# Weight slots filled out of turn, one split moved to the DVE, and an unpermuted sum at the end of a hybrid SSM, attention and MoE block

## The chip, the core and the metric

The kernel runs on one core of a Trainium2 chip. The metric is the device time of one execution in microseconds (us), as the median of several runs. TensorE is called PE in the profile (its weight loads PEld), VectorE DVE, ScalarE ACT, GpSimd POOL, SyncE SP. SP issues nearly all transfers here, in one queue.

## The reference, cut to what matters

One layer works on 272 tokens (16 meta tokens and 256 of input) of width 1024: a diagonal state-space branch and a sliding-window attention branch, both gated, are added to the stream; then a mixture of 32 experts with the top 4 for each token, and a last norm.

```python
proj = hn @ w_in[layer]                      # u, q, k, v and two gates
y = s5_ssm(u, ...); z = gelu(y); ssm_out = z * sigmoid(z @ w_glu + b_glu)
attn_out = sliding_window_attention(q, k, v, sinks)
h = h + (sigmoid(g_ssm) * (ssm_out @ w_br_ssm) + sigmoid(g_attn) * (attn_out @ w_br_attn)) @ w_out
...
gu = xb @ w_gate_up[e] + b_gate_up[e]        # 1024 x 2048 for each expert
g, up = clipped halves of gu
hid = g * sigmoid(1.702 * g) * (up + 1.0)
y = hid @ w_down[e] + b_down[e]              # 1024 x 1024 for each expert
...
return rmsnorm(h, norm_final)[:, N_META:]
```

Everything is float32. The weights of one expert are 8 MB (gate and up) and 4 MB (down), so 32 experts read 384 MB.

## The kernel before, in words

**The ring.** All weights go through one ordered list, `ring.todo`, into slots of 1024 KB (2048 floats on each of 128 partitions). First come single blocks (w_in, w_glu, w_br_ssm, w_br_attn, w_out), then the experts' units of four slots each: two units of gate and up for each expert (rows for k = 0 to 3 and 4 to 7), and one unit of down, which stands behind the gate and up units of the next expert. The order of units is therefore expert 0 (two), expert 1 (two), down of expert 0, expert 2 (two), down of expert 1, and so on. `pump` issues the head of the list as soon as there are free slots for it; a unit may be filled in one transfer of four slots, in pairs that lie beside each other in a "quad", or singly into two or more slots that stand alone. `done` gives a slot back when its last reader has been issued, and the transfer that refills it waits on SP for that reader. `retire` takes a slot out of the ring. With `patient` set, a unit waits for a whole quad; `most = 2` forbids that.

**The slots.** `r0` gives five slots (four of them later a quad, printed as r), and the quads ZScgtX, QYWgt and ws four each. Three slots stand alone in memory that other stages use: `s_acc` (in aA, where `acc` lies afterwards, opened in turn 8 of the block loop), `s_y` (late_, where the experts' outputs `ys` lie afterwards, opened in turn 15), and one more in aA, opened in turn 22. `s_acc` and `s_y` are retired after the block loop; the third stays in the ring. Before the change `s_acc` holds a block of w_br_ssm and then the rows for k = 2 of expert 0, the third one the rows for k = 3, and `s_y` a block of w_br_attn and then a row of expert 1's second unit.

**The block loop** (turns n = 0 to 41) works off 40 blocks: 8 each of the second gate, w_glu, w_br_ssm, w_br_attn and w_out. Each block's weights are split in two float32r parts: `hi` (ACT) copies, `lo` (L928) subtracts, and PE multiplies with both. The turns 0 to 13 also carry the steps of the attention: `scores` on PE, `normalise` of the step before and `maxima` on DVE, `exps` on ACT, `transposes` of the step before on PE with copies on ACT, `values` on PE. `bias_parts` (turns 0 to 2) splits the experts' bias into three bf16 parts on ACT, with a subtraction on DVE (L1024) between them. Program order in a turn sets the order on each engine.

**The experts.** For each expert, PE runs `gate_up` (k = 0 to 7, 32 products in pairs of column halves), then `down` of the expert before. Within `gate_up`, `mid(k)` places `hid_T` of the expert before, every second expert a `combine` of a pair of experts into `acc`, and steps of `group`, a generator that gathers the tokens of the next pair (`gather`, four steps) and makes its gate matrix (`gates_T`). For expert 0 every `mid(k)` takes one step of `group(0)`, of which two were taken before.

**The order of columns.** w_gate_up and w_down are read so that columns in the MoE stay in a permuted order ("p (n c)" against "p (c n)"): `down` turns the order back when it copies its result from PSUM (L1439, L1440), and the last stage writes its result through permuted views (L1526, L1527). The weights of the last norm are spread over the partitions by two products in PSUM (`nf_banks`, L1509) in the last expert's `gate_up`.

**The end.** `down(31)` has `combine_one` for the pair's first half in its turns c = 1 and c = 3 (two products, two adds into `acc`), and a second time for the other half after it. Then come squares (ACT), root (DVE, POOL), weigh (DVE), scale (ACT and DVE) and the stores.

Of the kernel before, what the change touches and what calls it, by code (L numbers as in the profile page):

```python
# [93 lines left out]


class Ring:
# [4 lines left out]
    def __init__(self, eng):  # L101
        self.eng = eng
        self.todo, self.held, self.free, self.used, self.patient, self.most = [], [], [], 0, False, 4

# [28 lines left out]
    def pump(self):  # L133
        while self.free and self.todo:
            u = self.todo[0]
            alone = [sl for sl in self.free if sl.quad is None]
# [8 lines left out]
            left = u.n - u.at  # L145
# [58 lines left out]
def hybrid_block(ctx: ExitStack, tc: tile.TileContext, x, meta, norm_mix, w_in, lam_re, lam_im, log_dt,  # L204
# [67 lines left out]
    for c in (6, 7):  # L272
        ring.add(dn_half(n_exp - 1, c))

# [926 lines left out]
    for n in range(B + 2):  # L1201
# [21 lines left out]
        if n == 0:  # L1223
            blocks[2].lo(G)
# [104 lines left out]
    keep_clock(bank("y", "idle"), b3[:, :128], b3[:, :416], 2)  # L1329
# [5 lines left out]
    keep_clock(bank("y", "idle"), b3[:, :128], b3[:, :416], 2)  # L1335
# [78 lines left out]

    cols2 = lambda t: t.rearrange("p (n c) -> p c n", c=4)
    rows2 = lambda t: t.rearrange("p (c n) -> p c n", c=4)

    def down(hT_, wc, selr, y, odd, mid=None, two=False):
# [20 lines left out]
        S.activation(rows2(y[:64, odd]), cols2(py[0][:64]), AF.Copy)  # L1439
        V.tensor_copy(rows2(y[64:, 1 - odd]), cols2(py[1][64:]))  # L1440

    def combine_one(gT, y, b, then=None):


        for t in range(2):
            pcs = [bank("y", "pc"), bank("t", "pc")]
            for hf in range(2):
                r = slice(64, 128) if hf != b else slice(0, 64)
                T.matmul(pcs[hf], gT[r, hf, t], y[r, hf], start=True, stop=True, tile_position=(r.start, 0))
            for hf in range(2):  # L1450
                cs_ = slice(512 * hf, 512 * hf + 512)
                V.tensor_tensor(acc[:, t, cs_], acc[:, t, cs_], pcs[hf], op=OP.add)
            if then:
                then(t)
            yield
# [3 lines left out]
    def combine(gT, y, then=None):  # L1459
        for t in range(2):  # L1460
            for hf in range(2):
# [3 lines left out]
                V.tensor_tensor(acc[:, t, cs_], (acc if started else xt)[:, t, cs_], pc, op=OP.add)  # L1465
# [13 lines left out]
    def group(e0, n):  # L1479
# [6 lines left out]
        if e0 == 0:  # L1486
            gates()
# [32 lines left out]
    def weigh(t, nf):  # L1520

        V.tensor_tensor(spare[t][:, :512], acc[:, t, :512], nf[0], op=OP.mult)

    def scale(t, nf):
# [7 lines left out]
    def last(nf):  # L1532
        for t in range(2):
            root(t)
            weigh(t, nf)
            scale(t, nf)
# [11 lines left out]
    more, nf = None, []  # L1548
    for e in range(n_exp + 1):
        f = e - 1  # L1550
        if e == n_exp - 1:
            nfr = pm.tile([128, 512], F32, tag="gT", name="nfr", bufs=3)
            for hf in range(2):
                S.dma_start(out=nfr[32 * hf:32 * hf + 1], in_=norm_final[512 * hf:512 * hf + 512].rearrange("(o d) -> o d", o=1))
        if e < n_exp:
# [3 lines left out]
            def mid(k):  # L1559
# [4 lines left out]
                if k == 4 and e == n_exp - 1:  # L1564
                    nf.extend(nf_banks())
# [3 lines left out]
            ring.patient, ring.most = 8 < e < 29, 4 if e < 29 else 2  # L1569
# [7 lines left out]
        if f >= 0:  # L1577
            if f % 2 == 0:
                assert ring.idle(s_y) or f
# [3 lines left out]
            def mid_d(c):  # L1583
                if e == n_exp - 1 and c == 3:
                    HID[e] = hid_T(HID[e])
                if e == n_exp and c in (1, 3):
                    next(one, None)

            if e == n_exp:
                one = combine_one(GT[f - 1], Y[f - 1], 0)  # L1590
# [14 lines left out]
    def sums(t):  # L1605
        if t == 0:
            return
        for tt in range(2):
            for hf in range(2):
                squares(tt, hf)  # L1610
        root(0)
        for tt in range(2):
            weigh(tt, nf)
        root(1)
        for tt in range(2):
            scale(tt, nf)

    assert list(GT) == [n_exp - 2]
    for _ in combine_one(GT.pop(n_exp - 2), Y.pop(n_exp - 2), 1, sums):
        pass  # L1620
# [3 lines left out]
    with tc.If(more > TS):  # L1624
# [35 lines left out]
        nf = nf_banks()  # L1660
# [3 lines left out]
        last(nf)  # L1664
# [33 lines left out]
```

## Time and profile before

| what | value |
|---|---|
| median of 3 runs | 1251.13 us (1249.76 to 1251.34) |
| profiled execution, its own time | 1247.98 us |
| its span, first to last instruction | 1246.1 us |
| mean granted PE clock | 0.987 |
| busy: PE, DVE, ACT, POOL | 95%, 36%, 19%, 5% |
| read from HBM | 443.32 MB |
| chain that ended last | PE 68%, DMA 22%, DVE 7%, ACT 1% |

The times are in microseconds from the span's start. The span falls into the state-space stage (to about 160), the block loop (160 to 317), the routing (317 to 322), and the experts (322 to 1232) with the tail behind them. Busy times of PE are modelled, so a wait of PE is read from the idle time that a row names in brackets, and from what the row says ended it.

### The profile page before, as it was taken

To read this page: it belongs to the slowest core of one execution; us is meant where nothing else is said; L and a number is where in the kernel's file an instruction comes from. 1 tells how busy PE (TensorE), PEld (TensorE's weight loads), DVE (VectorE), ACT (ScalarE), POOL (GpSimd) and SP (SyncE) were. 2 spreads that over 40 slices of the span, in tenths; PEclk is the share of its full clock that TensorE was granted. 3 is DMA by queue.
4 is the path that set the end of the run, shared out by engine and by line. 5 is a ranking of instruction groups with operands and counts; after the bars stand their busy time and mean duration, and the time that the engine had idled before them with its cause. 6 is when DMAs were issued, how large, how long until landed. Compare 5 with 4: busy or idle time off the path is not lost.

```text
span 1246.1 us, 16786 instructions
## 1 busy us (share of the span) xinstructions
PE 1178.6 (95%) x7152; PEld 594.8 (48%) x7153; DVE 451.5 (36%) x1002; ACT 231.5 (19%) x482; POOL 59.7 (5%) x93
## 2 busy tenths in 40 slices
PE   8989989999999999999998999999999999898996
PEld 6868878899433333334333333333333333333331
DVE  4979467776331222312121222122131212121223
ACT  3353466654100000000000000000000000000002
POOL 3009100000000000000000000000000000000000
PEclk9999999999999999999999999999999999999998
DMA  7934454786799999999999999999999999999993
GB/s 183 253 71 137 137 168 155 148 320 264 316 416 429 430 430 427 432 429 434 431 433 432 432 432 433 429 433 433 430 432 435 430 430 436 431 430 434 423 430 152
DMA packets 78559, 447.24 MB, mean 359 GB/s; under 512 B 22616, under 2 KB 58700, under 8 KB 60176
## 3 DMA queue, kind: packets, MB, share of 16 engines
q1 hardware_dynamic: 77820, 445.40, 88.1%
q8 instruction: 58, 0.95, 0.3%
q0 software_dynamic: 512, 0.45, 0.2%
q10 hardware_dynamic: 148, 0.27, 0.1%
q14 instruction: 21, 0.17, 0.0%
HBM read 443.32 MB, written 2.79 MB: 358 GB/s over the span
## 4 chain that ended last, share of the span: by engine, by line
PE 68%; DMA 22%; DVE 7%; ACT 1%; issue 1%; POOL 0%; SPq 0%; DVEq 0%; ACTq 0%
PE pgt L1388 14%; PE py L1433 13%; PE pup L1388 12%; DMA ZScgtX<-in_w_gate_up_dram 11%; DMA r<-in_w_gate_up_dram 9%; PE pg L1361 6%; PE pc L1463 4%; PE pu L506 3%; PE pu L949 2%; PE pu L950 2%; PE pu L951 2%; PE pu L496 2%; DMA ZScgtX<-in_w_down_dram 2%; PE pt L1409 1%; PE sc L1038 1%
## 5 line engine op out<-in xcount | busy, mean ns | idle before, releaser
L1362 DVE TENSOR_TENSOR xw<-pg,nfB 128x256 f32<-128x256 f32 x64 | 27.1, 424 | 214.3 <-PE pg L1361 214.3
L1399 DVE TENSOR_SCALAR gs<-pgt 128x512 f32<-128x512 f32 x32 | 22.0, 686 | 212.9 <-PE pgt L1388 212.9
L1361 PEld LDWEIGHTS pg<-aA,xt 128*128 128x128 f32 x512 | 62.6, 193 | 55.1 <-issue 55.1
L1440 DVE COPY late__1943<-py 64x512 f32<-64x512 f32 x32 | 22.2, 695 | 175.3 <-ACT late__1943 L1439 173.0
L1388 PE MATMUL pgt<-r,xw 128*64 128x512 f32 x284 | 74.4, 602 | 4.6 <-DMA r<-in_w_gate_up_dram 4.6
L1361 PE MATMUL pg<-aA,xt 128*128 128x128 f32 x512 | 74.4, 289 | 2.7 <-DVE aA L1351 2.3
L1388 PE MATMUL pup<-r,xw 128*64 128x512 f32 x284 | 73.0, 592 | 0.0
L1388 PE MATMUL pgt<-ZScgtX,xw 128*64 128x512 f32 x240 | 64.0, 612 | 8.0 <-DMA ZScgtX<-in_w_gate_up_dram 8.0
L1433 PE MATMUL py<-ws,hT 128*64 128x512 f32 x276 | 64.5, 620 | 7.4 <-DMA ws<-in_w_down_dram 6.9
L949 PE MATMUL pu<-kr,wh 128*128 128x256 f32 x240 | 69.4, 289 | 0.0
L951 PE MATMUL pu<-kr,wl 128*128 128x256 f32 x240 | 67.6, 282 | 0.2 <-DVE wl L928 0.2
L950 PE MATMUL pu<-kr,wh 128*128 128x256 f32 x240 | 67.6, 282 | 0.0
L1388 PE MATMUL pgt<-QYWgt,xw 128*64 128x512 f32 x256 | 67.3, 605 | 0.0
L1388 PE MATMUL pup<-QYWgt,xw 128*64 128x512 f32 x256 | 65.7, 592 | 0.0
L1433 PE MATMUL py<-QYWgt,hT 128*64 128x512 f32 x224 | 53.2, 627 | 10.9 <-DMA QYWgt<-in_w_down_dram 10.9
L1388 PE MATMUL pup<-ZScgtX,xw 128*64 128x512 f32 x240 | 63.4, 606 | 0.0
L1439 ACT ACTIVATE late__1943<-py 64x512 f32<-64x512 f32 x32 | 18.9, 590 | 228.8 <-PE py L1433 228.8
L1411 ACT ACTIVATE hT<-pt 128x512 f32<-128x512 f32 x32 | 19.1, 597 | 221.3 <-PE pt L1409 221.3
L1463 PE MATMUL pc<-late__1943,gT 128*128 128x512 f32 x120 | 58.3, 618 | 0.0
L1378 ACT ACTIVATE gT<-pt 128x512 f32<-128x512 f32 x16 | 9.6, 597 | 256.1 <-PE pt L1377 256.1
L1388 PE MATMUL pgt<-ws,xw 128*64 128x512 f32 x216 | 57.1, 607 | 0.0
L1433 PE MATMUL py<-ZScgtX,hT 128*64 128x512 f32 x252 | 56.3, 593 | 0.3 <-DMA ZScgtX<-in_w_down_dram 0.3
(363 smaller groups left out, 1764.2 us busy)
## 6 DMA issues: line engine op xcount, KB each, us to landing
r<-in_w_gate_up_dram SPq DMA_DIRECT2D x10, 4096.0 KB, 29.7
QYWgt<-in_w_gate_up_dram SPq DMA_DIRECT2D x10, 4096.0 KB
ws<-in_w_gate_up_dram SPq DMA_DIRECT2D x10, 4096.0 KB, 29.4
ZScgtX<-in_w_gate_up_dram SPq DMA_DIRECT2D x9, 4096.0 KB
QYWgt<-in_w_gate_up_dram SPq DMA_DIRECT2D x12, 2048.0 KB, 23.0
r<-in_w_gate_up_dram SPq DMA_DIRECT2D x12, 2048.0 KB, 22.7
ZScgtX<-in_w_gate_up_dram SPq DMA_DIRECT2D x12, 2048.0 KB, 20.2
ws<-in_w_down_dram SPq DMA_DIRECT2D x6, 4096.0 KB, 23.3
```

The lines of the kernel that those rows point to most:

```text
L496: T.matmul(pu[:, t], x_[:, 4 * self.h + k, c:c + 128], y_[:, k], start=(self.h + t + p + k == 0), skip_group_check=True, stop=(self.h == 1 ...
L506: T.matmul(pu, x_[:, k], y_[:, k, c:], start=(p + k == 0), stop=(p == len(pairs) - 1 and k == 7))
L949: T.matmul(pu, self.a[:, k], hi[:, k], start=(k == 0), stop=False)
L950: T.matmul(pu, self.a[:, k], lo[:, k], start=False, stop=False)
L951: T.matmul(pu, self.b[:, k], hi[:, k], start=False, stop=(k == 7))
L1361: T.matmul(pg[:, j], xt[:, t, 128 * (k + j):128 * (k + j) + 128], oh[:, t], start=(t == 0), stop=(t == 1))
L1362: V.tensor_tensor(xe[:, k:k + 2], pg, nfB[:, k:k + 2, None].to_broadcast([128, 2, n]), op=OP.mult)
L1388: T.matmul(p_[64 * hf:64 * hf + 64].rearrange("p (n c) -> p n c", c=4), lhs, half_of(rhs[:, c:c + D], hf), start=False, stop=(k == 7), til ...
L1399: V.tensor_scalar(gv, turned(pg), LIMIT, None, op0=OP.min)
L1433: T.matmul(py[pp][64 * pp:64 * pp + 64], lhs, rhs[:, 512 * hf:512 * hf + 512], start=(c == -1), stop=(c == 7), tile_position=(0, 64 * pp), ...
L1440: V.tensor_copy(rows2(y[64:, 1 - odd]), cols2(py[1][64:]))
L1463: T.matmul(pc, gT[:, hf, t], y[:, hf], start=True, stop=True)
```

## The change

The edits, in the order of the program:

- The ring remembers slots that are used once more before they are retired (`once`: `s_acc` and `s_y`) and a unit far down the list (`far`, the fifth unit of expert weights, which is the down unit of expert 0). When the list's head is an expert unit and a `once` slot is free, the far unit's last missing row is loaded into it at once; when the list comes to that unit, these rows are skipped.
- The subtraction of `bias_parts` is issued a turn later, just before `lo`, and block 2's `lo` runs on the DVE, where it ran on POOL.
- The third lone slot is kept as `s_n` and retired at expert 9; `patient` and transfers of four slots end at expert 27 instead of 29.
- Between the routing's products four and six filler products (`keep_clock`) stand where there were two and two.
- `down` copies its result unpermuted; the first `combine` permutes the residual stream instead; the last stage has no permuted views any more.
- `gates()` and the first `gates_of` of expert 0 come four steps later.
- The last norm's weights are spread by `norm_rows` in expert 22 into `nfb`, in SBUF, in the memory of `s_n`.
- At the end, the products for both halves of the last pair add up in four PSUM banks (`add_list`): the first half's at c = -1 and c = 3 of `down(31)`, the second's behind it, with one set of adds into `acc`.

```diff
@@ Ring.pump
-        while self.free and self.todo:
+        while self.todo:
             u = self.todo[0]
+            if isinstance(u, Unit):
+                for sl in [x for x in self.once if x in self.free]:
+                    i = self.far.n - 1 - len(self.far.pre)
+                    self.eng.dma_start(out=sl.ap, in_=self.far.src(i, 1))
+                    self.far.pre[i] = sl
+                    self.free.remove(sl)
+                    self.once.remove(sl)
+                if u.at in u.pre:
+                    self.held.append(u.pre[u.at])
+                    u.at += 1
+                    if u.at == u.n:
+                        self.todo.pop(0)
+                    continue
+            if not self.free:
+                return
...
-            left = u.n - u.at
+            left = u.n - u.at - len(u.pre)
...
+    ring.far = [u for u in ring.todo if isinstance(u, Unit)][4]
@@ bias_parts
         if q < 2:
-            V.tensor_tensor(bf, bf, bp[:, q], op=OP.subtract)
             return
@@ block loop
         if n == 0:
-            blocks[2].lo(G)
+            blocks[2].lo()
+        if 1 <= n < 3:
+            V.tensor_tensor(bf, bf, bp[:, n - 1], op=OP.subtract)
         if n > 1 and at(1):
             at(1).lo()
...
             s_acc = ring.slots([aA(0, U_)])[0]
+            ring.once.append(s_acc)
         if n == N + 1:
             s_y = ring.slots([late_])[0]
+            ring.once.append(s_y)
...
-            ring.slots([aA(8 * L + 768, U_)])
+            s_n = ring.slots([aA(8 * L + 768, U_)])[0]
...
-    keep_clock(bank("y", "idle"), b3[:, :128], b3[:, :416], 2)
+    keep_clock(bank("y", "idle"), b3[:, :128], b3[:, :416], 4)
...
-    keep_clock(bank("y", "idle"), b3[:, :128], b3[:, :416], 2)
+    keep_clock(bank("y", "idle"), b3[:, :128], b3[:, :416], 6)
@@ down
-        S.activation(rows2(y[:64, odd]), cols2(py[0][:64]), AF.Copy)
-        V.tensor_copy(rows2(y[64:, 1 - odd]), cols2(py[1][64:]))
-
-    def combine_one(gT, y, b, then=None):
...
+        S.activation(y[:64, odd], py[0][:64], AF.Copy)
+        V.tensor_copy(y[64:, 1 - odd], py[1][64:])
+
+    def add_list(pcs, t, gT, y, b):
+        for hf in range(2):
+            r = slice(64, 128) if hf != b else slice(0, 64)
+            T.matmul(pcs[t, hf], gT[r, hf, t], y[r, hf], start=(b == 0), stop=(b == 1), tile_position=(r.start, 0),
+                     skip_group_check=True)
@@ group
         if e0 == 0:
+            for _ in range(4):
+                yield
             gates()
@@ the last norm's weights
-    def nf_banks():
-        nf = [bank("g", "nf"), bank("u", "nf")]
+    nfb = aA(8 * L + 768, D)
+    def norm_rows():
+        nfr = aA(8 * L + 768 + D, 512)
         for hf in range(2):
-            T.matmul(rows2(nf[hf]), cv["ones"][32 * hf:32 * hf + 1], cols2(nfr[32 * hf:32 * hf + 1]), start=True, stop=True)
-        return nf
+            S.dma_start(out=nfr[32 * hf:32 * hf + 1], in_=norm_final[512 * hf:512 * hf + 512].rearrange("(o d) -> o d", o=1))
+        for hf in range(2):
+            pn = bank("t", "nf")
+            T.matmul(pn, cv["ones"][32 * hf:32 * hf + 1], nfr[32 * hf:32 * hf + 1], start=True, stop=True)
+            S.activation(nfb[:, 512 * hf:512 * hf + 512], pn, AF.Copy)
@@ scale
-        S.activation(cols2(o[:, :512]), rows2(spare[t][:, :512]), AF.Copy, scale=rsf[:, t:t + 1])
-        V.scalar_tensor_tensor(cols2(o[:, 512:]), rows2(acc[:, t, 512:]), rsf[:, t:t + 1], rows2(nf[1]),
-                               op0=OP.mult, op1=OP.mult)
+        S.activation(o[:, :512], spare[t][:, :512], AF.Copy, scale=rsf[:, t:t + 1])
+        V.scalar_tensor_tensor(o[:, 512:], acc[:, t, 512:], rsf[:, t:t + 1], nfb[:, 512:], op0=OP.mult, op1=OP.mult)
@@ expert loop
+                if k == 1 and e == max(0, n_exp - 10):
+                    norm_rows()
...
-            ring.patient, ring.most = 8 < e < 29, 4 if e < 29 else 2
+            if e == 9:
+                ring.retire(s_n)
+            ring.patient, ring.most = 8 < e < 27, 4 if e < 27 else 2
...
-                if e == n_exp and c in (1, 3):
-                    next(one, None)
+                if e == n_exp and c in (-1, 3):
+                    add_list(pcs, int(c > 0), GT[f - 1], Y[f - 1], 0)
```

## Rows read from the trace of the kernel before

**Rows 1.** Stretches: us, busy us by engine, clock, DMA share, GB/s last.

```profile
325.00:335.00 10.00, 8.77 (x48) 3.98 (x46) 3.49 (x14) 1.40 (x2) 0.00 (x0) 1.00 0.69 272
335.00:341.00 6.00, 6.00 (x30) 1.99 (x28) 0.00 (x0) 0.48 (x1) 0.00 (x0) 1.00 0.23 48
350.00:352.00 2.00, 2.00 (x14) 0.79 (x12) 0.00 (x0) 0.60 (x1) 0.00 (x0) 1.00 0.83 229
380.00:640.00 260.00, 257.31 (x1220) 96.84 (x1218) 67.02 (x141) 19.41 (x33) 0.00 (x0) 0.99 1.01 430
640.00:1140.00 500.00, 469.19 (x2182) 174.76 (x2180) 114.57 (x236) 35.36 (x60) 0.00 (x0) 0.98 1.00 432
1140.00:1222.00 82.00, 82.00 (x376) 28.96 (x372) 18.12 (x32) 5.97 (x11) 0.00 (x0) 1.00 0.99 424
```

**Rows 2.** Timeline, PE in the routing, the experts and the tail.

```profile
319.12 0.53 PE L364 MATMUL idle<-b 96*128 96x416 bf16 x2
...
321.77 0.46 PE L1361 MATMUL pg<-aA,xt 128*128 128x128 f32 x2 [0.84 <-DVE aA L1351]
...
332.80 0.46 PE L1377 MATMUL pt<-ct,aA 128*128 128x128 f32 x2 [1.23 <-DVE aA L1351]
...
1139.65 0.65 PE L1388 MATMUL pgt<-ZScgtX,xw 128*64 128x512 f32 x2 [2.09 <-DMA ZScgtX<-in_w_gate_up_dram]
...
1206.76 2.04 PE L1509 MATMUL nf<-nfr,ct 1*128 1x512 f32 x4
...
1222.40 1.94 PE L1433 MATMUL py<-ZScgtX,hT 128*64 128x512 f32 x8 [0.26 <-DMA ZScgtX<-in_w_down_dram]
```

**Rows 3.** Timeline of SP's queue around expert 0.

```profile
314.85 0.33 SPq L162 DMA_DIRECT2D ws<-in_w_down_dram  x1
328.66 0.33 SPq L162 DMA_DIRECT2D r<-in_w_gate_up_dram  x1
338.82 0.33 SPq L162 DMA_DIRECT2D QYWgt<-in_w_gate_up_dram  x1
...
375.30 0.33 SPq L162 DMA_DIRECT2D r<-in_w_gate_up_dram  x1
```

**Rows 4.** Timeline of DVE, POOL and ACT around the loop's first turns.

```profile
158.56 1.22 DVE L928 TENSOR_TENSOR kr<-r,kr 128x1024 fp32r<-128x1024 f32 x1
...
163.88 2.40 POOL L928 TENSOR_TENSOR wl<-r,wh 128x1024 fp32r<-128x1024 f32 x1 [33.80 <-ACT wh L925]
...
164.22 2.07 DVE L1138 TENSOR_TENSOR sm<-sm,snk 112x2 f32<-112x2 f32 x1
...
168.19 0.44 ACT L1145 ACTIVATE late__1943<-sc,sm 112x240 f32<-112x240 f32 x1
...
170.13 0.96 DVE L1024 TENSOR_TENSOR aA<-aA 128x768 f32<-128x768 f32 x1 [2.51 <-ACT aA L1022]
...
171.39 0.66 DVE L1152 TENSOR_TENSOR late__1943<-late__1943,sm 112x480 f32<-112x480 f32 x1
```

**Rows 5.** Timeline, PE and PEld in the first turns.

```profile
172.20 0.48 PE L1174 MATMUL pt<-ct,late__1943 112*128 112x112 f32 x3 [2.19 <-DVE late__1943 L1152]
...
189.97 0.13 PEld L1187 LDWEIGHTS pu<-QYWgt,aA 128*64 128x64 f32 x1 [0.90 <-ACT QYWgt L1176]
```

**Rows 6.** A stretch of the first turns; the granted clock stands third from the end.

```profile
172.50:176.50 4.00, 4.00 (x20) 3.61 (x19) 1.73 (x7) 3.35 (x10) 0.00 (x0) 0.57 0.01 4
```

**Rows 7.** Timeline of DVE, ACT and POOL in the tail.

```profile
1222.59 0.69 DVE L1440 COPY late__1943<-py 64x512 f32<-64x512 f32 x1 [5.64 <-ACT late__1943 L1439]
...
1235.86 0.63 ACT L1514 ACTIVATE sq<-aA 128x512 f32<-128x512 f32 x1
...
1237.17 2.50 ACT L1526 ACTIVATE ws<-ws,rsf 128x512 f32<-128x512 f32 x2
...
1237.73 2.05 DVE L1527 SCALAR_TENSOR_TENSOR ws<-aA,rsf,nf 128x512 f32<-128x512 f32 x2
1237.89 0.55 POOL L1518 TENSOR_TENSOR rsf<-ssf,nhalf 128x1 f32<-128x1 f32 x1 [0.75 <-DVE ssf L1517]
```

More of the change, by code (lines that the diff above doesn't have):

```diff
@@ L93, in __init__ @@
         self.n, self.src, self.at = n, src, 0
+        self.pre = {}
 class Ring:
@@ L103, in __init__ @@
         self.todo, self.held, self.free, self.used, self.patient, self.most = [], [], [], 0, False, 4
+        self.far, self.once = None, []
     def add(self, parts):
@@ L1518, in root, with weigh, scale, last @@
         G.tensor_tensor(rsf[:, t:t + 1], ssf[:, t, 0:1], nhalf, op=OP.pow)
-    def weigh(t, nf):
-        V.tensor_tensor(spare[t][:, :512], acc[:, t, :512], nf[0], op=OP.mult)
-    def scale(t, nf):
+    def weigh(t):
+        V.tensor_tensor(spare[t][:, :512], acc[:, t, :512], nfb[:, :512], op=OP.mult)
+    def scale(t):
         o = spare[t][:, D:]
-        S.activation(cols2(o[:, :512]), rows2(spare[t][:, :512]), AF.Copy, scale=rsf[:, t:t + 1])
-        V.scalar_tensor_tensor(cols2(o[:, 512:]), rows2(acc[:, t, 512:]), rsf[:, t:t + 1], rows2(nf[1]),
-                               op0=OP.mult, op1=OP.mult)
+        S.activation(o[:, :512], spare[t][:, :512], AF.Copy, scale=rsf[:, t:t + 1])
+        V.scalar_tensor_tensor(o[:, 512:], acc[:, t, 512:], rsf[:, t:t + 1], nfb[:, 512:], op0=OP.mult, op1=OP.mult)
         (S if t else nc.sync).dma_start(out=ov[:, t, :512], in_=o[:, :512])
         nc.sync.dma_start(out=ov[:, t, 512:], in_=o[:, 512:])
-    def last(nf):
+    def last():
         for t in range(2):
             root(t)
-            weigh(t, nf)
-            scale(t, nf)
+            weigh(t)
+            scale(t)
     groups = {e: min(2, n_exp - e) for e in range(0, n_exp, 2)}
@@ L1547, in hybrid_block @@
     imax = cp.tile([128, 1], I32, name="imax")
-    more, nf = None, []
+    more = None
     for e in range(n_exp + 1):
         f = e - 1
[L1551 to L1554, printed above, removed]
         if e < n_exp:
@@ L1578, in hybrid_block @@
             if f % 2 == 0:
-                assert ring.idle(s_y) or f
                 Y[f] = ys[f // 2 % 2]
@@ L1585, in mid_d @@
                     HID[e] = hid_T(HID[e])
-                if e == n_exp and c in (1, 3):
-                    next(one, None)
+                if e == n_exp and c in (-1, 3):
+                    add_list(pcs, int(c > 0), GT[f - 1], Y[f - 1], 0)
             if e == n_exp:
-                one = combine_one(GT[f - 1], Y[f - 1], 0)
+                pcs = {(t, hf): bank("gu"[t], "pc") for t in range(2) for hf in range(2)}
             down(HID.pop(f), ring_d(f == n_exp - 1), selrow(f), Y[f - f % 2], f % 2, mid_d, f == n_exp - 1)
@@ L1602, in hybrid_block @@
             more = nc.values_load(imax[0:1, 0:1], min_val=0, max_val=NT)
[L1605 to L1616, printed above, removed]
-    assert list(GT) == [n_exp - 2]
-    for _ in combine_one(GT.pop(n_exp - 2), Y.pop(n_exp - 2), 1, sums):
-        pass
+    assert list(GT) == [n_exp - 2]
+    gT, y = GT.pop(n_exp - 2), Y.pop(n_exp - 2)
+    for t in range(2):
+        add_list(pcs, t, gT, y, 1)
+        for hf in range(2):
+            cs_ = slice(512 * hf, 512 * hf + 512)
+            V.tensor_tensor(acc[:, t, cs_], acc[:, t, cs_], pcs[t, hf], op=OP.add)
+    for t in range(2):
+        for hf in range(2):
+            squares(t, hf)
+    root(0)
+    for t in range(2):
+        weigh(t)
+    root(1)
+    for t in range(2):
+        scale(t)
     gT = pm.tile([128, 2, 2, 128], F32, tag="gT", name="gT", bufs=3)
@@ L1659, in hybrid_block @@
                     combine(gT, ys[0])
-        nf = nf_banks()
         for t in range(2):
@@ L1663, in hybrid_block @@
                 squares(t, hf)
-        last(nf)
+        last()
     close(hp2)
```

21 lines of the change are left out of this document (5 added, 16 removed).

## The prediction

> **What bounds the kernel now.** I read the page's chain first: PE has 68% of it and DMA 22%, which does not say which of them sets the end. The stretches do. From 380 to 1140 the DMA engines are full (share 1.00 to 1.01, 430 and 432 GB/s) while PE has gaps; earlier, around expert 0, they are not: 272, 48 and 229 GB/s in three stretches between 325 and 352 [rows 1]. So the end of the stream of expert weights is set by how early it becomes full and by the bytes left then; a slot of 1024 KB takes 2.43 us at 432 GB/s. Next I read PE's waits. Its last real wait for weights is 2.09 us at 1139.65; from there to 1222 it is busy for 82 of 82 us, and at 1222.40 it waits 0.26 us more, for the last down rows [rows 1, 2]. PE was thus held by the stream up to 1139.65, catches up in the last experts, and meets the stream's end just there: if the stream moves, both move.
>
> So there are three places where the change can matter: what lies ahead of the full stream, how many bytes are under way by then, and what follows the last bytes.
>
> **Step 1, the loop's first turns.** POOL's `lo` of block 2 takes 2.40 us from 163.88, and the DVE's tiny L1138 that starts beside it takes 2.07 us and ends as POOL ends [rows 4]; its like costs some 0.15. Then the DVE waits 2.51 us for ACT before the bias subtraction L1024 (0.96), and `normalise`, L1152, stands behind it and ends at 172.05 [rows 4]. PE's `transposes` wait 2.19 us for it [rows 5], and after this gap PE has a granted clock of 0.57 for four microseconds [rows 6], that is the 1.2 GHz level for 1.7 us' worth of lost work (4.0 x 0.43).
>
> After: L1138 gives back 1.9 us, and the gelu steps, the tanh behind them and the exps all come by so much sooner: the exps start near 166.3 instead of 168.19 [rows 4]. `lo` takes 1.22 us on the DVE [rows 4], in the time in which it waits for them. `normalise` has no bias subtraction ahead of it any more and ends some 2.1 us behind the exps' start, near 168.4 instead of 172.05. PE finishes block 1 near 170.0, so the 2.19 us wait is gone, and with it the fall of the clock. The subtraction now runs in turn 1 near 171, when ACT is long done with its input, and in turn 2 just ahead of `lo` of block 3: which I expect to end near 176.2, 0.3 us after PE wants it. Net on PE: 2.19 + 1.70 - 0.3 = 3.6 us. A little further PE waits 0.90 us for ACT's copies at 189.97 [rows 5]; ACT's chain comes 4.7 us sooner by the same count (exps of turn 3 near 178.4 instead of 183.1), so this wait vanishes too: 3.6 + 0.9 = 4.5 us. From there to the routing the chain of waits runs through PE, so 4.5 us reach the experts. Bounds: 2.2 (the gap alone) and 4.7 (ACT's chain).
>
> **Step 2, the ring.** I followed `pump` through both orders. Up to the ws quad (issue at 314.85) both have 20 slots of expert rows under way: the new order loads down rows of expert 0 into `s_acc` and `s_y`, but leaves the third lone slot empty from turn 22 to 34, since a single lone slot is not filled while an even row is due. So nothing is gained there. The gain comes in expert 0. Before, its rows for k = 2 and 3 lie in the lone slots, one retired and one not usable alone, so pairs come free after k = 1, 5 and 7: the first two are the issues at 328.66 and 338.82 [rows 3]. After, k = 2 and 3 lie in a pair of QYWgt, so there is an issue after each of k = 1, 3, 5 and 7, and the rest moves up by one.
>
> Also, expert 0's gate matrix comes at k = 6 instead of k = 2, when the DVE has long made it: PE's 1.23 us wait at 332.80 goes [rows 2], and every issue from k = 3 on comes 1.2 us sooner.
>
> The lost time of the stream is then, at 432 GB/s: before, 325 to 335, 10 x 160 / 432 = 3.7 us; 335 to 341, 6 x 384 / 432 = 5.3 us; 350 to 352, 0.9 us; 10.0 us in all [rows 1]. After (times without the shift of step 1): the first 3.7 stay. The issue after k = 3 comes near 333.3, before the pair ahead of it has landed near 335, so the 5.3 and the 0.9 go. But the two once-slots give nothing back later: 18 slots are issued from 328.66 to the middle of `down(0)`, the last 16 of them are through by 335.0 + 16 x 2.43 = 373.9, and the next pair comes free when expert 2 is through k = 1, at 375.30 [rows 3] less 1.2, that is 374.1; with some 1.6 us until bytes flow (as after 338.82: 2.2 us to 341 at 48 GB/s or a little more [rows 1, 3]) the stream loses 1.8 us. Net 10.0 - 3.7 - 1.8 = 4.5; I take 4.3, since the last two units of the chain stand close to their slots too. Bounds: 1.2 (only the gate matrix's wait, all the rest lost in the new gap) and 6.2 (no new gap). Behind that PE frees slots faster than the stream fills them, as before.
>
> **Step 3, the tail.** PE loses the 2.04 us of L1509 in the last expert [rows 2], worth little since PE then waits for the stream. With pieces of two slots from expert 27 on, PE is about 0.9 us nearer the stream when the last pair lands. Against that, the first half's products now stand at c = -1 of `down(31)`, ahead of all its rows, and need the copy L1440 of the expert before, which ended at 1223.28, just after PE was ready at 1222.14 [rows 2, 7]: a new wait of about 1.4 us, with all of `down(31)` queued behind it. Together PE ends about 0.3 us sooner relative to the stream. Then: ACT's permuted write L1526 takes 1.25 us each (2.50 for two), an unpermuted one of that size 0.63 (L1514); the second one cannot start before POOL's root ends at 1238.44, so one of them counts: 0.6 us; the DVE's pair (2.05 in all) shortens beside it [rows 7]. Net 0.9 us. Bounds: 2.0 gained, and 2.5 lost if the wait is followed by a fall of the clock like the one in [rows 6].
>
> **At nothing.** The filler products fit into waits of PE for the DVE in the routing, the later of them 0.84 us; with no cover six more at half of 0.53 us each would cost 1.6 us [rows 2]. `norm_rows` makes PE wait for a fresh transfer in expert 22; by an estimate from the 2.2 us of 338.82 to 341 it costs 2 to 5 us if nothing hides it. The stream's backlog does: an expert's 12 slots take 29.1 us, of which PE is busy 469 of 500 [rows 1], so it regains 1.8 us in each of the nine experts that follow. The permuted first `combine` and the retired `s_n` fall into the full stream as well; with `patient` that slot lay idle.
>
> [...] The change issues five more weight transfers (the pieces of two slots in experts 27 and 28). Before, the stretch made mostly of pairs runs at 430 GB/s and the one made mostly of quads at 432 [rows 1]: over 260 us, nine experts with three more transfers each, that is 1.2 us, so 0.2 us for five, which I leave out. [...]
>
> **The sum.** 4.5 + 4.3 + 0.9 = 9.7 us. The profiled execution took 1247.98 us, 3.15 below the median of the runs shown; it becomes 1238.3, and the median 1251.1 - 9.7 = 1241.4.
>
> **The rivals.**
>
> A. The ring gives almost nothing: pairs come free sooner, but the stream then runs dry at expert 2's first pair. For it: the 18 slots end within a microsecond of that issue. Against: even dry for 1.8 us it keeps more than half. Then 4.5 + 1.2 + 0.9: 1244.5 us. Chance 0.15.
>
> B. Another chain takes PE's wait in the first turns: the DVE now has `lo` of block 2 and the late subtractions, and PE wants block 3's `lo` close to when it is made. For it: the DVE has one more piece of 1.22 us there, and two subtractions stand behind more work. Against: it sat idle for 2.51 us [rows 4]. With 2.2 left, 2.2 + 4.3 + 0.9: 1243.7. Chance 0.10.
>
> C. The tail's new wait costs 1.4 us, and a fall of the clock behind it 1.7, less 0.6: 2.5 lost. 1251.1 - 4.5 - 4.3 + 2.5 = 1244.8. Chance 0.05.
>
> D. On the other side: the split transfers of experts 27 and 28 cost the stream what a transfer that starts on dry engines costs, about 2 us each between issue and flow (338.82 to 341 [rows 1, 3]). Five make 10 to 11 us: 1252. It decides from about 1.9 us a transfer. Against it stand the 430 GB/s of the stretch made of pairs; but no row shows the switch itself late in the stream, so it keeps 0.12 (0.07 slower, 0.05 the same). [...]
>
> The forecast has 0.58.
>
> **How the numbers follow.** Faster by over 0.2% (2.5 us, about what a measurement of this kernel tells from no change): the forecast, A, B and C, 0.88. Same 0.05, slower 0.07. The upper bounds together (4.7 + 6.2 + 2.0) give 1238.2, less 1.4 for the spread of the runs 1236.8; A and B together (2.2 + 1.2 + 0.9) give 1246.8, with that spread 1248.2. The range is 1236.8 to 1248.0, and leaves out D.
>
> **What would show it.** Step 1: no POOL in L928, a short first L1138, no clock below 1.00 between 165 and 190, the routing near 312 to 313. Step 2: SP issues after each odd k of expert 0, the DMA share near 1.00 from there but for a dip near expert 2's first pair, no 1.23 us wait at L1377. Step 3: a wait of PE at the end sums ahead of `down(31)`, ACT's last scale near 0.6 us each. The forecast is wrong if the stream's rate falls below 430 GB/s after 1080, if PE's waits in the loop only move to another turn, or if the stream has a new dry stretch longer than 2 us.

## The result, and the profile after

The kernel after takes 1242.97 us (median of 4 runs, 1241.71 to 1245.23), the kernel before 1250.97 beside it; the ratio is 0.9939, 95% interval [0.9925, 0.9953], so 7.6 us less (5.9 to 9.4; the two medians alone differ by 8.0). The forecast was 9.7 us less, 1241.4, and its range 1236.8 to 1248.0 holds the result.

The profiled execution of after took 1245.23 us, the slowest of its four, while that of before was faster than the median of its kernel. Their spans, 1243.5 and 1246.1, are therefore only 2.6 us apart. A second trace of the unchanged after, taken with the experiments (experiment 5), has a span of 1239.7. Where the two differ, both are shown.

The stretches of after, columns as in [rows 1]; the first answers to [rows 6], the second is the routing:

```profile
172.50:176.50 4.00, 4.00 (x35) 3.88 (x34) 3.86 (x10) 3.95 (x12) 0.00 (x0) 1.00 0.02 6
314.00:322.00 8.00, 7.94 (x37) 4.71 (x37) 3.54 (x19) 0.67 (x4) 0.96 (x2) 0.57 1.02 436
325.00:335.00 10.00, 10.00 (x54) 4.09 (x54) 3.49 (x14) 0.00 (x0) 0.00 (x0) 1.00 0.67 249
335.00:341.00 6.00, 6.00 (x34) 2.23 (x32) 1.15 (x2) 2.51 (x3) 0.00 (x0) 1.00 1.01 431
350.00:352.00 2.00, 2.00 (x14) 1.17 (x12) 0.13 (x1) 0.00 (x0) 0.00 (x0) 1.00 1.09 451
374.00:376.00 2.00, 2.00 (x12) 0.76 (x10) 0.00 (x0) 0.60 (x1) 0.00 (x0) 1.00 0.89 303
378.00:382.00 4.00, 4.00 (x22) 1.31 (x20) 0.00 (x0) 0.00 (x0) 0.00 (x0) 1.00 0.94 336
380.00:640.00 260.00, 256.98 (x1226) 96.59 (x1224) 68.95 (x142) 19.43 (x33) 0.00 (x0) 1.00 1.01 430
640.00:1140.00 500.00, 473.54 (x2216) 176.16 (x2213) 114.36 (x235) 37.18 (x63) 0.00 (x0) 0.99 1.00 431
```

The dry stretch from 335 to 341 is gone (431 GB/s for 48) and so is the one at 350; in their place stands a shallower one near expert 2's first pair (303 and 336 GB/s). The full stream has the rate that it had. The clock between 172.5 and 176.5 is 1.00 where it was 0.57. But in this execution it is 0.57 in the routing, where before had none.

The DVE in the loop's first turns, timeline of after, to set against [rows 4]:

```profile
166.06 0.16 DVE L1158 TENSOR_TENSOR sm<-sm,snk 112x2 f32<-112x2 f32 x1
...
167.47 1.22 DVE L949 TENSOR_TENSOR wl<-r,wh 128x1024 fp32r<-128x1024 f32 x1
...
169.62 0.66 DVE L1172 TENSOR_TENSOR late__1943<-late__1943,sm 112x480 f32<-112x480 f32 x1
...
172.15 0.96 DVE L1246 TENSOR_TENSOR aA<-aA 128x768 f32<-128x768 f32 x1
```

POOL has no row from 155 to 190. The tiny row takes 0.16 us for 2.07, `lo` of block 2 takes 1.22 on the DVE, `normalise` ends at 170.28 for 172.05 (at 169.34 in the second trace; the forecast had 168.4), and the subtraction comes one turn later. The wait for ACT's copies of [rows 5] is shorter, but it has not gone (timeline of PEld):

```profile
186.65 0.13 PEld L1207 LDWEIGHTS pu<-QYWgt,aA 128*64 128x64 f32 x1 [0.48 <-ACT QYWgt L1196]
```

SP's queue, to set against [rows 3]:

```profile
311.91 0.42 SPq L181 DMA_DIRECT2D ws<-in_w_down_dram  x1
327.51 0.33 SPq L181 DMA_DIRECT2D r<-in_w_gate_up_dram  x1
332.18 0.33 SPq L181 DMA_DIRECT2D QYWgt<-in_w_gate_up_dram  x1
335.61 0.33 SPq L181 DMA_DIRECT2D r<-in_w_gate_up_dram  x1
339.78 0.33 SPq L181 DMA_DIRECT2D QYWgt<-in_w_gate_up_dram  x1
...
373.06 0.33 SPq L181 DMA_DIRECT2D r<-in_w_gate_up_dram  x1
```

The issue at 314.85 has come 2.9 us sooner; behind 327.51 there are three more issues by 340 where there was one.

The tail, to set against [rows 7] (PE's row is the first half's products):

```profile
1218.19 1.85 PE L1467 MATMUL pc<-late__1943,gT 64*128 64x512 f32 x4 [0.47 <-ACT late__1943 L1459]
...
1228.30 0.59 ACT L1459 ACTIVATE late__1943<-py 64x512 f32<-64x512 f32 x1 [10.16 <-PE py L1453]
...
1232.94 0.94 POOL L1544 TENSOR_TENSOR rsf<-ssf,nhalf 128x1 f32<-128x1 f32 x1 [917.20 <-DVE ssf L1543]
...
1233.91 0.72 ACT L1552 ACTIVATE QYWgt<-QYWgt,rsf 128x512 f32<-128x512 f32 x1 [0.35 <-POOL rsf L1544]
...
1234.26 0.99 POOL L1544 TENSOR_TENSOR rsf<-ssf,nhalf 128x1 f32<-128x1 f32 x1 [0.38 <-DVE ssf L1543]
...
1235.28 0.75 DVE L1553 SCALAR_TENSOR_TENSOR QYWgt<-aA,rsf 128x512 f32<-128x512 f32 x1 [0.44 <-POOL rsf L1544]
...
1236.03 0.41 ACTq L1554 DMA_DIRECT2D out_dram<-QYWgt  x1
```

Two rows of before for the same places, ACT's copy behind PE's last down product and the issue of the last store:

```profile
1231.93 0.59 ACT L1439 ACTIVATE late__1943<-py 64x512 f32<-64x512 f32 x1 [9.37 <-PE py L1433]
...
1239.70 0.41 ACTq L1529 DMA_DIRECT2D out_dram<-ws  x1
```

ACT's write takes 0.72 us for 1.25 (foretold 0.63) and the DVE's 0.75 for some 1.03. What was not foretold: POOL's roots take 0.94 and 0.99 us for some 0.55. From PE's last down product to the issue of the last store it is 7.73 us (1228.30 to 1236.03); before it was 7.77 (1231.93 to 1239.70).

### The profile page after: what moved, and what is told of

The parts are those of the page before. It is cut to its first block, busy times and chain, and to the rows that moved or that the text cites. A ratio compares the mean times of both kernels' runs of the same rounds, so it can differ in the third digit from the quotient of the medians.

```text
span 1243.5 us, 16802 instructions
## 1 busy us (share of the span) xinstructions
PE 1178.6 (95%) x7158; PEld 595.8 (48%) x7159; DVE 448.0 (36%) x999; ACT 231.9 (19%) x484; POOL 58.3 (5%) x92
## 4 chain that ended last, share of the span: by engine, by line
PE 73%; DMA 22%; DVE 3%; ACT 1%; issue 1%; POOL 0%; ACTq 0%; SPq 0%; DVEq 0%; POOLq 0%
PE pgt L1412 14%; PE py L1453 13%; PE pup L1412 12%; DMA ZScgtX<-in_w_gate_up_dram 11%; DMA r<-in_w_gate_up_dram 7%; PE pg L1385 5%; PE pu L527 4%; PE pc L1476 4%; DMA ZScgtX<-in_w_down_dram 3%; PE pu L970 3%; PE pu L971 2%; PE pu L972 2%; PE pu L517 2%; PE pt L1433 1%; PE sc L1148 1%; PE sc L1058 1%
## 5 line engine op out<-in xcount | busy, mean ns | idle before, releaser
L1453 PE MATMUL py<-ws,hT 128*64 128x512 f32 x296 | 67.5, 606 | 10.3 <-DMA ws<-in_w_down_dram 10.3
L1412 PE MATMUL pgt<-QYWgt,xw 128*64 128x512 f32 x264 | 70.4, 612 | 0.0
L1412 PE MATMUL pup<-QYWgt,xw 128*64 128x512 f32 x264 | 68.7, 599 | 0.0
L1412 PE MATMUL pup<-ws,xw 128*64 128x512 f32 x216 | 55.4, 592 | 0.0
L1479 DVE TENSOR_TENSOR aA<-aA,pc 128x512 f32<-128x512 f32 x56 | 38.5, 687 | 46.9 <-PE pc L1476 46.9
```

Source lines behind the costliest of these rows:

```text
L1412: T.matmul(p_[64 * hf:64 * hf + 64].rearrange("p (n c) -> p n c", c=4), lhs, half_of(rhs[:, c:c + D], hf), start=False, stop=(k == 7), til ...
L1453: T.matmul(py[pp][64 * pp:64 * pp + 64], lhs, rhs[:, 512 * hf:512 * hf + 512], start=(c == -1), stop=(c == 7), tile_position=(0, 64 * pp), ...
L1479: V.tensor_tensor(acc[:, t, cs_], acc[:, t, cs_], pc, op=OP.add)
```

## The experiments

The theory: the loop gives 4 to 5 us, the ring with the gate matrix 3 to 4, the sums nothing; where PE's clock falls is partly chance. The rivals: R1, most of the gain is that chance; R2, the ring loses its gain again in the new gap, or PE's wait only moves to another turn; and, for the tail, that its new wait costs what it seems to. Intervals are in us of gain over before, worked out from the interval of the ratio.

**1. The loop alone.** In the kernel before:

```diff
         if q < 2:
-            V.tensor_tensor(bf, bf, bp[:, q], op=OP.subtract)
             return
...
-            blocks[2].lo(G)
+            blocks[2].lo()
+        if 1 <= n < 3:
+            V.tensor_tensor(bf, bf, bp[:, n - 1], op=OP.subtract)
```

> The kernel before with step 1 alone (lo of block 2 on the DVE, the two bias subtractions one turn later). My theory: the loop really ends about 4.5 us sooner (4.9 by the two traces, by the SP issues of block 20), and all but the chance of where the clock falls reaches the end: 3.5 to 5 us less, 1246.5. In its trace POOL has no row from 155 to 190, the DVE's row after the first lo takes under 0.3 us, and the issue that stood at 314.85 stands near 311. Rival R1 (the gain of the whole change is mostly chance of the clock): the routing's clock falls and eats it, at most 2 us less. Rival R2 (PE's wait only moves to another turn): the issue stands within 1 us of 314.85 and the time is within 1 us.

Measured: 1246.36 us, ratio 0.9967 [0.9956, 0.9979], a gain of 4.1 us (2.6 to 5.5). Its stretch, and SP's row of the timeline:

```profile
172.50:176.50 4.00, 4.00 (x36) 3.87 (x34) 3.86 (x10) 3.93 (x13) 0.00 (x0) 1.00 0.03 10
```

```profile
324.56 0.33 SPq L162 DMA_DIRECT2D r<-in_w_gate_up_dram  x1
```

The issue that stood at 328.66 [rows 3] stands 4.1 us sooner, and the medians give 4.1 us at the end. (The spans of the two traces, 1246.1 and 1243.4, differ by 2.7, so one pair of traces does not show that all of it arrives.) R2 has no place in the loop. Nor has R1: in nine traces of kernels with this edit the clock never falls between 172 and 180; of the five without it (before and four variants) it falls there in four.

**2. The ring alone.** In the kernel before, the change's lines in Ring and Unit and these:

```diff
             s_acc = ring.slots([aA(0, U_)])[0]
+            ring.once.append(s_acc)
...
             s_y = ring.slots([late_])[0]
+            ring.once.append(s_y)
```

> The kernel before with the ring's part alone (the two slots used once are filled with the last rows of the fifth unit). My theory: the dry stretch from 335 to 341 goes (more than 400 GB/s in it), a new gap of about 2 us stands at expert 2's first pair, and 2.5 to 3.5 us remain: 1248. Rival R2 (the new gap gives the whole back): within 1 us of before. Rival R1 (chance): no verdict beyond 1 us, and the two traces' stretches differ elsewhere.

**3. The gate matrix alone.** In the kernel before:

```diff
         if e0 == 0:
+            for _ in range(4):
+                yield
             gates()
```

> The kernel before with the gate matrix of the first two experts four steps later, and nothing else. My theory: PE's 1.23 us wait at 332.80 goes, and since the pairs come free sooner by that, the stream gains 0.8 to 1.2 us: 1250. Rival: the wait comes back at the next product or is hidden by the slots that are taken only in pairs: within 0.3 us of before.

**4. After without the ring.** In the kernel after, the lines of experiment 2 and those in Ring and Unit taken out again:

```diff
-            ring.once.append(s_acc)
...
-            ring.once.append(s_y)
```

> The kernel after with the ring's part undone: the two slots used once are filled in turn again; the later gate matrix, the loop, the sums and the fillers stay. My theory: the dry stretch near 332 to 337 comes back with some 4 to 5 us and the gap at expert 2's first pair (1.6 to 1.8 us) goes: 2 to 3 us slower than the kernel after, 1245.5. Rival R2 (the ring is worth only what it gave alone or less): 1 to 2 us slower. Rival: the gate matrix pays only with the ring, then 3 us or more slower.

**5. After again**, unchanged.

> The kernel after, unchanged, timed in more rounds beside its variants, and with a second trace. Measured so far: loop alone 4.1 us (ratio 0.9967), ring alone 1.9 (0.9985), gate matrix alone 0 (1.0002), the sums' part alone 0.6 (0.9995); together 6.6, the whole change 8.0. My theory: the parts add up, the whole is 7 to 8 us, and the fall of the clock in the routing (0.50 from 314.9 to 321.7 in the first trace) is not there in each execution. Rival: the whole is worth 2 us more than its parts, because the gate matrix pays only together with the ring: 8 us or more.

Measured, all four beside before: the ring alone 0.9985 [0.9975, 0.9995], 1.9 us (0.6 to 3.1); the gate matrix alone 1.0002 [0.9993, 1.0011], nothing; after again 0.9934 [0.9920, 0.9947], 8.3 us; after without the ring 0.9962 [0.9948, 0.9976], 4.8 us. So in its place in the change the ring is worth 3.5 us, and the slowest run of after again (1244.15) lies below the fastest without the ring (1245.72). What the stream loses is seen in one stretch of 100 us around expert 0. Before, then the first trace of after:

```profile
300.00:400.00 100.00, 95.34 (x546) 47.84 (x545) 31.18 (x84) 13.88 (x34) 0.96 (x2) 1.00 0.93 389
```

```profile
300.00:400.00 100.00, 97.81 (x536) 47.65 (x534) 29.31 (x81) 12.53 (x29) 0.96 (x2) 0.97 0.95 394
```

The ring alone, then the gate matrix alone:

```profile
300.00:400.00 100.00, 95.33 (x552) 49.05 (x552) 32.65 (x86) 14.21 (x35) 0.96 (x2) 1.00 0.96 398
```

```profile
300.00:400.00 100.00, 96.34 (x560) 49.75 (x560) 33.05 (x87) 14.61 (x35) 0.96 (x2) 1.00 0.95 391
```

After again, then after without the ring:

```profile
300.00:400.00 100.00, 97.39 (x543) 46.52 (x542) 29.76 (x82) 12.01 (x28) 0.96 (x2) 1.00 0.97 404
```

```profile
300.00:400.00 100.00, 97.39 (x546) 47.18 (x547) 29.76 (x82) 12.37 (x29) 0.96 (x2) 1.00 0.95 390
```

Against 432 GB/s the last four lose 7.9, 9.5, 6.5 and 9.7 us; before lost 10.0. So, by single traces, the ring alone saves 2.1, the gate matrix alone 0.5, both 3.5, and with the gate matrix in place the ring saves 3.2. The first trace of after loses 8.8, since there the clock falls in the routing and expert 0 comes later. The ring alone still has a dry stretch before its second pair has landed, because that pair comes 6.7 us behind the first (337.04 behind 330.30 on SP's queue; in after 4.7, 332.18 behind 327.51), and the new gap at expert 2 beside it:

```profile
336.00:340.00 4.00, 4.00 (x22) 1.40 (x20) 0.00 (x0) 1.12 (x1) 0.00 (x0) 1.00 0.69 223
378.00:386.00 8.00, 8.00 (x40) 2.76 (x38) 0.00 (x0) 0.60 (x1) 0.00 (x0) 1.00 0.97 344
```

By the same sum these are 1.9 and 1.6 us. After again loses 1.2 from 372 to 380 (369 GB/s there). The gap that the prediction put at 1.8 is real, and it doesn't take the whole gain: R2 falls here, too. (The ring alone also pays 1.1 us at the program's end, as experiments 10 and 11 will show: it has 462 SP instructions, and its span ends 7.7 us behind the last store's issue. Without that its 1.9 us would be 3.0.)

**6. The sums alone.** In the kernel after, all of the other parts undone (loop, ring, gate matrix, fillers, the pieces of experts 27 and 28). It keeps `norm_rows`, the retired `s_n` and, against before:

```diff
-        S.activation(rows2(y[:64, odd]), cols2(py[0][:64]), AF.Copy)
+        S.activation(y[:64, odd], py[0][:64], AF.Copy)
...
+                if e == n_exp and c in (-1, 3):
+                    add_list(pcs, int(c > 0), GT[f - 1], Y[f - 1], 0)
```

> The kernel after without its loop part, its ring, its later gates, its fillers and its pieces of two slots in experts 27 and 28: what remains is the unpermuted sums, the first half's products ahead of the last expert's down rows, the norm's rows copied in expert 22 and the slot retired at expert 9. My forecast gave this part 0.9 us (bounds 2.0 gained, 2.5 lost). By the two traces I now expect 0, from 0.6 lost to 0.6 gained: the shorter writes of ACT and the DVE (about 0.55 and 0.35 us each) against a new wait of about 1.4 us ahead of the down rows and POOL's root 0.4 us longer each. Rival: the tail gives its full 1 to 2 us, then the whole change's gain of 8.0 needs less from the loop and the ring. Second rival: it loses 2 us or more, by the new wait and a fall of the clock behind it.

Measured: 1249.65 us, ratio 0.9995 [0.9986, 1.0005], 0.6 us (0.6 lost to 1.8 gained). In its trace POOL's roots take 0.93 and 0.98 us. PE's last down product ends 14.1 us ahead of the span's end, as before (1231.93 to 1246.1). So the sums give nothing that the trace shows.

**7. The first half's products at c = 1.** In the kernel after:

```diff
-                if e == n_exp and c in (-1, 3):
-                    add_list(pcs, int(c > 0), GT[f - 1], Y[f - 1], 0)
+                if e == n_exp and c in (1, 3):
+                    add_list(pcs, int(c > 1), GT[f - 1], Y[f - 1], 0)
```

> The kernel after with the first half's products behind the second and the last down rows (c = 1 and 3, as before the change) instead of ahead of all (c = -1 and 3); the sums stay as in after. My forecast: at c = -1 PE waits about 1.4 us for ACT's copy, with all of the last expert's down rows behind it. My theory now: the last down rows come with the end of the stream in any case, so the wait is partly hidden: 0 to 1 us faster than after. Rival: PE is the one that is late there, and the whole wait comes back: 1.4 us faster. Second rival: the products at c = 1 stand between rows that have landed and cost their own 0.6 us: slower by it.

Measured: 0.9936 [0.9922, 0.9951], as after again. PE's row in its tail:

```profile
1215.38 1.94 PE L1453 MATMUL py<-ws,hT 128*64 128x512 f32 x8 [1.00 <-DMA ws<-in_w_down_dram]
```

Without the products ahead of them the down rows wait 1.00 us for their weights instead. The wait at c = -1 lies under the stream, and its place is worth nothing that these runs can tell.

**8. The fillers back at 2 and 2.** In the kernel after:

```diff
-    keep_clock(bank("y", "idle"), b3[:, :128], b3[:, :416], 4)
+    keep_clock(bank("y", "idle"), b3[:, :128], b3[:, :416], 2)
...
-    keep_clock(bank("y", "idle"), b3[:, :128], b3[:, :416], 6)
+    keep_clock(bank("y", "idle"), b3[:, :128], b3[:, :416], 2)
```

> The kernel after with the filler products in the routing back from 4 and 6 to 2 and 2. My forecast put them at nothing. If they are hidden: within 0.5 us of the kernel after, and the first real product of the routing starts as before its wait for the DVE. Rival: they keep the clock up, and without them it falls more often there: 1 to 2 us slower than the kernel after. Other rival: at half clock they take 1.57 and 2.24 us (first trace of after) and stand in the way of the gather: 0.5 to 1 us faster than the kernel after.

Measured: 0.9935 [0.9921, 0.9949], as after. PE's filler rows of after and, behind them, of after again:

```profile
316.33 1.57 PE L385 MATMUL idle<-b 96*128 96x416 bf16 x4
...
317.81 2.24 PE L385 MATMUL idle<-b 96*128 96x416 bf16 x6
```

```profile
314.81 0.88 PE L385 MATMUL idle<-b 96*128 96x416 bf16 x4
...
316.11 1.22 PE L385 MATMUL idle<-b 96*128 96x416 bf16 x6
```

At full clock they end ahead of the DVE and cost nothing; at the lower level (0.57 in that stretch of after) they take nearly twice as long and hold up the gather twice, by some 0.7 us each: once ahead of the products that the DVE waits for, and once ahead of its first product at 319.85. The fall in the routing is in one of the eight traces with the loop's edit and the sums. Only one of the eight has two and two fillers, so whether their number matters for the fall is not shown.

**9. The norm's row in PSUM.** In the kernel after:

```diff
+    nf = [bank("t", "nf"), bank("t", "nf")]
+    for hf in range(2):
+        T.matmul(nf[hf], cv["ones"][32 * hf:32 * hf + 1], ..., start=True, stop=True)
...
-        weigh(t)
+        weigh(t, nf)
```

> The kernel after, but the final norm's row is spread over the partitions by two products into two PSUM banks behind the last expert's sums (as before the change), and the DVE's weighing and scaling read it there, not in SBUF. In after POOL's two roots take 0.94 and 0.99 us beside the DVE's L1548, which has both inputs in SBUF; before, with one input in PSUM, they took 0.56 and 0.55 [rows 7]. My theory: it is the DVE's second SBUF input that holds POOL up: the roots take 0.55 to 0.6 us again, and the last store is issued 0.4 to 0.8 us sooner behind PE's last product of the down rows. Rival: POOL is held up by something else (the store's buffer, the place of the tile), the roots stay at 0.9 to 1.0 us and nothing changes. In the time either is below what the rounds can tell (0.8 us of 1243).

Measured: 0.9929 [0.9915, 0.9942]. POOL's and ACT's rows of its tail:

```profile
1224.73 0.59 ACT L1459 ACTIVATE late__1943<-py 64x512 f32<-64x512 f32 x1 [10.16 <-PE py L1453]
...
1229.38 0.56 POOL L1544 TENSOR_TENSOR rsf<-ssf,nhalf 128x1 f32<-128x1 f32 x1 [913.91 <-DVE ssf L1543]
...
1230.69 0.55 POOL L1544 TENSOR_TENSOR rsf<-ssf,nhalf 128x1 f32<-128x1 f32 x1 [0.75 <-DVE ssf L1543]
...
1232.02 0.40 ACTq L1554 DMA_DIRECT2D out_dram<-QYWgt  x1
```

The roots are short again, and from PE's last product to the last store's issue it is 7.29 us instead of 7.73. The time alone can't tell this.

**10. No pieces of two in experts 27 and 28**, and **11. eight tiny transfers more**. The first in the kernel after, the second in the kernel before:

```diff
-            ring.patient, ring.most = 8 < e < 27, 4 if e < 27 else 2
+            ring.patient, ring.most = 8 < e < 29, 4 if e < 29 else 2
```

```diff
+        if e == 10:
+            for i in range(8):
+                nc.sync.dma_start(out=idle8[0:1, 4 * i:4 * i + 4], in_=...)
```

> The kernel after with the pieces of four slots kept in experts 27 and 28, as before the change (six transfers fewer on SP's queue), all else as in after. Two things hang on it. Rival D of the prediction (each further transfer costs the stream about 2 us): then 10 to 12 us faster than after. My theory: the stream's rate does not change, and PE is about 0.9 us further from the stream's end, but a new point speaks for this version: in the kernels with over 460 SP instructions in the trace (after 468, ring alone 462, no ring 465) the span ends 7.4 to 7.7 us behind the issue of the last store, with four reads of instructions one behind the other on SP's queue of them, in those with under 460 (before 459, loop alone 458, gates alone 459, sums alone 454) 6.4 us, with three. With some 456 instructions here: 6.4 us, and in all 0 to 1 us faster than after. If the number of instructions is not the cause: 7.5 us behind the last issue, and 0 to 1 us slower.

> The kernel before with eight transfers of 16 bytes more, issued on SP's queue at expert 10 into a tile that nobody reads, so that SP has some 467 instructions instead of 459. The theory of the end (SP's instructions are read in pieces, and a program that ends just behind the start of a piece waits for one more read): the span ends 7.4 to 7.7 us behind the issue of the last store instead of 6.4, 1.1 us slower than before in all. Rival: the end depends on what the last transfers are or on the ring, then 6.4 us and the same time as before. By rival D of the prediction (each transfer costs about 2 us of the stream) it is 16 us slower.

Measured: without the pieces 0.9926 [0.9913, 0.9940]; with the tiny transfers 1.0067 [1.0053, 1.0081], 8.4 us slower (6.6 to 10.1). The reads of instructions at the end of the span (queue: packets, MB, share; from 1235.5, 1231 and 1250 us on), of after, of experiment 10 and of experiment 11:

```profile
q14 instruction: 4, 0.03, 1.3%
```

```profile
q14 instruction: 3, 0.02, 1.0%
```

```profile
q14 instruction: 4, 0.03, 1.0%
```

With 456 SP instructions there are three reads and the span ends 6.4 us behind the last store's issue (1231.40 to 1237.8); with 467 there are four and it is 7.5 us (1250.44 to 1257.9), as in after with 468 (1236.03 to 1243.5). In experiment 11 no other engine's instructions are more than in before, and in experiment 10 none are fewer than in after. So after pays 1.1 us at its end for having some more transfers than before.

Experiment 11 missed in its sum, since the transfers were not cheap where they stood (SP's row of the timeline, and a stretch behind it):

```profile
592.12 25.87 SPq L1558 DMA_DIRECT2D idle<-in_norm_final_dram  x8
```

```profile
615.00:620.00 5.00, 2.94 (x17) 0.97 (x14) 1.68 (x5) 0.59 (x1) 0.00 (x0) 1.00 0.40 118
```

The eight issues hold SP for 25.87 us, the weights' issues stand behind them, and the stream runs dry (118 GB/s for 5 us, 377 in the five ahead: 4.3 us). With the end that makes 5.4 of the 8.4; why each issue waits, and the rest, stay open.

Rival D of the prediction falls by experiment 10: six transfers fewer gave no 10 to 12 us but, against after again, 1.0 (the intervals overlap), and the traces show 1.1 at the end. The Trainium skill's page "DMA: Bandwidth & Descriptors", section "Anatomy of one DMA — SWDGE (gpsimd) path", gives a fixed 2.0 us for a transfer that GpSimd issues and puts most of it down to the wait for completion. These transfers are SP's, and no such cost for each of them is seen on the full stream.

**12. Experiments 9 and 10 together**, with the edits of both in the kernel after.

> The kernel after with the two things that the runs point to: pieces of four slots kept in experts 27 and 28 (456 SP instructions instead of 468; alone 0.9926 of before against 0.9934) and the final norm's row in two PSUM banks for the last weighing and scaling (POOL's roots 0.56 and 0.55 us instead of 0.94 and 0.99; alone 0.9929). My theory: the end of 6.4 us behind the last store's issue and the short roots come together: 1.1 + 0.4 us less than after, ratio to before 0.9922, 1241.8 us. Rival: both were the spread of the runs: 0.9934, 1243.2.

Measured: 1241.15 us (1238.80 to 1242.86), ratio 0.9923 [0.9910, 0.9937], 9.6 us less than before and the shortest time measured here. From PE's last product to the span's end it is 13.7 us (1223.35 to 1237.0); in after it was 15.2, before 14.2. Against after (0.9934) the intervals overlap; the 1.5 us is the trace's.

## Why the prediction was right, and where its sizes were off

Step 1 held. The forecast was 4.5, the part alone gave 4.1 (2.6 to 5.5), and its signs came: no POOL row, the short L1158, no wait at 172, no fall behind it. The term of 0.9 was too large: the wait for ACT's copies shrank from 0.90 to 0.48 and did not vanish. The 0.3 that block 3's `lo` was to cost PE stands in no row. So the rows give 2.19 + 1.70 + 0.42 = 4.3. The routing came 2.8 us sooner in the first trace and 4.3 in the second (PE's first fillers at 316.33 and 314.81, against the 319.12 of [rows 2]). One thing was missed: PE's wait of 1.3 us for ACT's `r` near 161, in before too, is sometimes followed by a fall of the clock and sometimes not (0.71 from 161 to 165 in after again; none in before or experiment 1). It is there in three of the nine traces with the loop's edit and in four of the five without, so I count it as spread between executions; that the edit leaves it alone isn't shown.

Step 2 held in its mechanism and order: issues behind each odd k, the dry stretch gone, no wait for the gate matrix, a new gap. Its size is 3.5 us by time and 3.5 by the stream's loss (1.2 in the trace with the fall in the routing), forecast 4.3. The 1.2 us put down to the gate matrix gave nothing alone; with the ring in place the stream saves 1.4 more than by the ring alone (3.5 less 2.1), which rests on single traces. The remark that the lower bound of 1.2 is "only the gate matrix's wait" was thus wrong in kind.

Step 3 is the step that failed. Forecast 0.9, it gave 0.0 by the trace, and the 1.1 us of the program's end came on top, which no step had. The PE part ("ends about 0.3 us sooner") was 0.0: from the last weight bytes to PE's last product it is 5.1 us before and 5.2 after (1226.8 to 1231.9, 1223.1 to 1228.3). The pieces of two slots, which were to bring PE 0.9 us nearer to the stream, do nothing there: without them (experiment 10) it is 5.1, too. The new wait came much as forecast, 0.47 us and another 0.7 inside the row of 1218.19 (1.85 us for 1.13 at c = 3), but experiment 7 shows that it doesn't count. Of ACT's write 0.5 us came, and POOL's roots took it back.

The terms at nothing held: the fillers (experiment 8) and, but for some tenths of a us, the split transfers' effect on the stream. There are six of them, not five, and one of the prediction's own signs of being wrong came by a hair, a rate below 430 GB/s after 1080. Before, then after:

```profile
1080.00:1200.00 120.00, 114.45 (x535) 42.78 (x536) 28.71 (x60) 8.24 (x14) 0.00 (x0) 1.00 1.00 431
```

```profile
1080.00:1200.00 120.00, 115.56 (x536) 41.86 (x534) 28.70 (x56) 8.84 (x15) 0.00 (x0) 1.00 1.00 429
```

Over these 120 us that is 0.6 us; experiment 10 has 430 there. `norm_rows` and `s_n` have no run of their own; experiment 6 contains them and lost nothing clear of noise.

The sum as measured: 4.1 + 3.5 + 0.0 - 1.1 = 6.5 us by parts (7.1 with the 0.6 of experiment 6), against 7.6 (5.9 to 9.4) and 8.3 (6.6 to 10.0) for the whole. What is left over is within the intervals of the parts, and is not explained further. All the sizes were too large: 0.4 in the loop, 0.8 in the ring, 0.9 in the tail and the 1.1 of the end, 3.2 in all. That the whole missed by only 2.1 can be luck or the intervals of the parts.

## What to carry to other kernels

Where a stream of weights sets the end, count its dry stretches in us of lost transfer; a slot filled out of turn is worth what the dry stretch loses less what the slot no longer gives back later, and here that sum came within 1 us. A stall in a tail costs nothing while the weights behind it have not landed; move its products elsewhere, as experiment 7 does, and look at what PE then waits for. Before many small steps are given to a queue, look at how many reads of its own instructions stand at the end of the program.

## What the hardware showed that was not expected

POOL's tiny root takes 0.94 to 0.99 us beside a DVE instruction with two inputs in SBUF and 0.55 to 0.56 beside the same with one in PSUM (experiment 9). The Trainium skill's page "GPSIMD Engine Reference", section "Specifications", says that POOL shares its way to SBUF with VectorE and contends with DVE instructions that have two SBUF inputs; the trace agrees. The prediction, which counted the DVE's gain of an unpermuted write, did not look at what moving the norm's weights from PSUM to SBUF does to POOL. In step 1 the same is seen the other way round: the DVE's tiny row took 2.07 us beside POOL's `lo` [rows 4] and 0.16 without it.

The end of the program depends on how SP's instructions fall into the pieces in which they are read: up to 459 of them in the trace three reads and 6.4 us behind the last store, from 462 on four and 7.4 to 7.7 us, in fourteen traces without an exception. The Trainium skill's page "Runtime: NRT & Kernel Launch", section "Instruction fetch mechanics", says that each engine reads its instructions in blocks while it executes, mostly hidden; at the end of this program nothing hides it, and the reads on this queue are of 8 KB, not of its 16 KiB.
